# Attention stage of a hybrid decoder layer: a second PSUM bank for the value products, with the transpose buffers on three banks in place of four

## The chip, the cores and the metric

The kernel runs on one core of one Trainium2 chip. The metric is the device time of one execution in microseconds. Each of the core's engines has its own queue and takes its instructions in the order of the program: TensorE (PE in the profile; PEld is its weight load), VectorE (DVE), ScalarE (ACT), GpSimd (POOL) and SyncE (SP, here only for issuing transfers). Semaphores make one engine wait for another. PE writes its results to PSUM, of which the program uses eight banks of 512 float32 columns on 128 partitions; VectorE and ScalarE read them from there.

## The reference

One decoder layer: a mixture of dilated-window attention and pooling, a gated MLP with a short convolution, a gated embedding, and a final norm. The change touches the attention alone, which reduces to this:

```python
def _dilated_branch(q, k, v, slopes, window, dil):
    ...
    s = jnp.einsum('bnqrhd,bnkrhd->bnrhqk', qb, kk,
                   preferred_element_type=jnp.float32)
    ...
    s = s - slopes[:, None, None] * dist
    s = jnp.where(valid[:, None, None], s, -jnp.inf)
    m = jnp.max(s, axis=-1, keepdims=True)
    e = jnp.exp(s - m)
    den = jnp.sum(e, axis=-1)
    o = jnp.einsum('bnrhqk,bnkrhd->bnqrhd', e, vv.astype(jnp.float32))
    ...
def _dilated_attention(q, k, v, slopes):
    outs, maxes, dens = [], [], []
    for window, dil in DIL_PATTERNS:
        o, m, d = _dilated_branch(q, k, v, slopes, window, dil)
    ...
    w = d * jnp.exp(m - jnp.max(m, axis=0, keepdims=True))
    w = w / jnp.sum(w, axis=0, keepdims=True)
    return jnp.sum(w[..., None] * o, axis=0)
```

There are 8 heads of width 64, 2048 tokens, and three patterns (window, dilation): (128, 1), (512, 4), (2048, 16).

## The kernel before

The program has three stages on one core: projections (`phase_project`), attention (`phase_attention`), and the rest (`phase_rest`: output projection, MLP, gated embedding, final norm). Float32 values are carried as a high and a low part in the type float32r, so most products are made two or three times.

**Steps.** Attention runs over 128 steps: 8 heads of 16 query tiles of 128 tokens. Each step has a *near* part (dilation 1, 256 keys) and a *far* part that covers the two wider patterns together (128 to 512 keys). Four steps make a group, in which the far part has 512, 384, 256 and 128 keys in this order. Two heads make a pair.

**Order.** The order on every engine is written by hand. In tick s the loop goes through the list `CFG["ord"]`, and an entry with lag n works on step s-n. What matters here, in the order of the list:

- N, near scores of step s, two matmuls (L572, L573) into one half of the bank `sn`. Both halves belong to one tile and alternate by step.
- S, after the last step of a pair, the transposes of its statistics (`mix_stats`, or `last_near` for the last pair).
- o (lag 7), in every second tick: ScalarE copies half of the value result, `ev` (L659).
- F, far scores of step s, two matmuls (L561, L562) into `sf`, which has two banks.
- h (lag 2): ScalarE copies the transposed weights of step s-2 to their high part, `pth` (L613).
- nm: VectorE's near minimum of step s (L577).
- p (lag 7), in every second tick: the *fold*. VectorE adds the two halves of the value result (L660).
- fm: VectorE's far minimum (L583).
- l (lag 2): VectorE subtracts to get the low part of step s-2, `ptl` (L617).
- T (lag 1): PE transposes the exponentials of step s-1, three to six blocks of 128 columns (L600), into `tp`.
- V and W (lag 6): value products into the bank `o`: the far ones of a group (L642) in two ticks, then its near ones (L628) in two ticks. Every second tick starts a new result in `o`.
- ne, fe: ScalarE's exponentials of step s.

Instructions stand on their engine in this order, so on PE a tick reads N, F, T, V, W, and on VectorE nm, p, fm, l.

**PSUM.** The eight banks of the stage: `sn` one, `sf` two, `tp` four (two buffers of 1024 columns, of which a step uses up to 768), `o` one. A pool with `bufs=2` gives its tiles two places in turn, and whoever writes into a place waits until the tile before in that place has been read. Inside one tile the recording layer makes a write wait for earlier reads, and reads for earlier writes, as far as it takes them to touch the same memory. The statistics of a pair are transposed into a `tp` buffer (`tps`), and so are those of the last pair (`tpn`, `tpf`); these are then copied to SBUF by VectorE (L769, L771, L806) or ScalarE (L817).

Of the kernel before, what the change touches and what calls it, by code (L numbers as in the profile page):

```python
# [10 lines left out]
F32 = mybir.dt.float32  # L11
# [3 lines left out]
PSUM = bass.MemoryType.PSUM  # L15
DRAM = bass.MemoryType.DRAM

P = 128
# [5 lines left out]
NPAIR = H // 2  # L24
FF = 2816
NF = FF // P
CH = 512
# [27 lines left out]
def rdma(nc, dst, src):  # L55
    nc.sync.dma_start(fp(dst) if dst.dtype == F32R else dst, fp(src) if src.dtype == F32R else src)
# [429 lines left out]
def phase_attention(tc, g, mx, near_b, far_b):  # L486
# [3 lines left out]
    nc = tc.nc  # L490
    NS = H * NQ
    with ExitStack() as ctx:
        sb = ctx.enter_context(tc.tile_pool(name="b_sb", bufs=1, reuse_waits="tile"))
        ps_n = ctx.enter_context(tc.tile_pool(name="b_n", bufs=1, space=PSUM, reuse_waits="tile"))
        ps_f = ctx.enter_context(tc.tile_pool(name="b_f", bufs=2, space=PSUM, reuse_waits="tile"))
        ps_t = ctx.enter_context(tc.tile_pool(name="b_t", bufs=2, space=PSUM, reuse_waits="tile"))
        ps_o = ctx.enter_context(tc.tile_pool(name="b_o", bufs=1, space=PSUM, reuse_waits="tile"))

        heads, steps, groups, pairs = {}, {}, {}, {}

        def load_qk(h):
            t = heads[h] = Shared()
            pr, e = h // 2, h % 2
            rows = slice(DH * e, DH * e + DH)
            t.qhh = sb.tile([P, S], F32R, tag=f"qhh{e}", bufs=1, name=f"qhh{h}")
            t.qll = sb.tile([P, S], F32R, tag=f"qll{e}", bufs=1, name=f"qll{h}")
            t.qr = t.qhh.rearrange("p (c r) -> p r c", r=4)
            t.qlr = t.qll.rearrange("p (c r) -> p r c", r=4)
            t.ks = sb.tile([P, NCH, 4, P], F32R, tag=f"ks{e}", bufs=1, name=f"ks{h}")
            t.nb = sb.tile([P, 256], F32, tag=f"nb{e}", bufs=1, name=f"nb{h}")  # L510
            t.fb = sb.tile([P, 512], F32, tag=f"fb{e}", bufs=1, name=f"fb{h}")
            loads = []
            for half in range(2):
                hs = slice(half * DH, half * DH + DH)
                loads.append((t.qhh[hs], g.qh[pr][rows]))
                loads.append((t.ks[hs], (g.kh if half == 0 else g.kl)[pr][rows]))
                loads.append((t.qll[hs], g.ql[pr][rows]))
            loads += [(t.fb, far_b[h]), (t.nb, near_b[h])]
            return loads
# [5 lines left out]
        def load_v(pr, which, q):  # L525

            v = sb.tile([P, 4, 2, P], F32R, tag=which, bufs=4 + (which == "v1"), name=f"{which}_{pr}_{q}")
            vals[pr, which, q] = v
            src = near_v[:, 4 * q : 4 * q + 4, pr, :] if which == "v1" else far_v[q, :, :, pr, :]
            return v.rearrange("p b h d -> p b (h d)"), src  # L530
# [63 lines left out]

        def turn(s):
            st = steps[s]
            st.tp = ps_t.tile([P, 1024], F32, tag="t", name="tp")
            for b in range(2 - st.nb, 2 + st.nf):
                bs = slice(b * P, (b + 1) * P)
                nc.tensor.transpose(st.tp[:, bs], st.ee[:, bs], g.ident)  # L600
# [96 lines left out]
        def stats(s):  # L697
            if (s + 1) % (2 * NQ) == 0:
                pr = s // (2 * NQ)
                if pr < NPAIR - 1:  # L700
                    mix_stats(nc, g, mx, ps_t, pr, pairs[pr])
                else:
                    last_near(nc, g, mx, ps_t, pairs[pr])

        def mix(s):
            for pr in range(NPAIR - 1):
# [14 lines left out]
                    if d == CFG["m"][2] + CFG["m"][3] * c + CFG["m"][5]:  # L721
                        mix_store(nc, g, mx, nc.gpsimd, nc.gpsimd, pr, pairs[pr], c)()

        near_bank = []
        sel = mx.tile([8, NCH, 2, DH], F32R, tag="sel", name="sel")
        for c in range(NCH):
            nc.vector.tensor_copy(sel[:, c], g.ident[:8, c : 8 : NCH, None].to_broadcast([8, 2, DH]))
        with tc.manual_schedule(engines=set(EN.values())):
            for dst, src in load_qk(0):
                rdma(nc, dst, src)  # L730
            for q in range(4):
                for which in ("v3", "v1"):
                    rdma(nc, *load_v(0, which, q))
            queue = []
            stages = {
                "F": far_scores, "N": near_scores, "fm": far_max, "nm": near_max, "fe": far_exp, "ne": near_exp,
                "T": turn, "h": high, "l": low, "V": values, "W": values_b, "S": stats, "M": mix, "o": fold, "p": folded, "B": begin
            }
            for s in range(NS + 10):
                if s < NS:  # L740
                    h, n = divmod(s, NQ)
                    if n == 1 and h + 1 < H:
                        queue += load_qk(h + 1)
                    if queue:
                        rdma(nc, *queue.pop(0))
                    for pr in range(1, NPAIR):
                        if s - 2 * NQ * (pr - 1) in V_STEPS:
                            rdma(nc, *load_v(pr, *V_STEPS[s - 2 * NQ * (pr - 1)]))
                if s == NS + 2:
                    last_far(nc, g, mx, ps_t, pairs[NPAIR - 1])  # L750
                    pieces = pairs[NPAIR - 1].pieces = last_weights(nc, mx, pairs[NPAIR - 1])
                for nm, lag in CFG["ord"]:
                    if 0 <= s - lag < NS or nm == "M":
                        stages[nm](s - lag)
                for _ in range({NS + 3: 3, NS + 4: 2, NS + 5: 1}.get(s, 0)):
                    next(pieces)
# [1 line left out]
    return pairs[NPAIR - 1]  # L758


def mix_stats(nc, g, sb, psum, pr, pt):

    tp = psum.tile([P, 1024], F32, tag="t", name="tps")
    nc.tensor.transpose(tp[:64, :P], pt.st1.rearrange("p a e n -> p (a e n)"), g.ident)
    far = tp[:16, CH:].rearrange("p (c r) -> p r c", r=4)
    for r in range(4):
        nc.tensor.transpose(far[:, r, :], pt.st3[:, r].rearrange("p a e i -> p (a e i)"), g.ident)
    sx = sb.tile([64, P], F32, tag="sx", name="sx")
    nc.vector.tensor_copy(sx, tp[:64, :P])  # L769
    sy = sb.tile([16, CH], F32, tag="sy", name="sy")  # L770
    nc.vector.tensor_copy(sy, tp[:16, CH:])  # L771
    pt.sx, pt.sy = sx, sy


# [18 lines left out]

def last_near(nc, g, sb, psum, pt):

    near = psum.tile([P, 1024], F32, tag="t", name="tpn")
    for a in range(2):
        for m in range(4):
            nc.tensor.transpose(
                near[:8, a * CH + m * P : a * CH + (m + 1) * P],  # L800
                pt.st1[:, a].rearrange("p e (i m) -> p m e i", m=4)[:, m],
                g.ident,
            )
    pt.near = [sb.tile([16, CH], F32, tag="sy", name="nr")[:8], sb.tile([P, CH], F32, tag="m3", bufs=1, name="nr")[:8]]
    for a in range(2):
        nc.vector.tensor_copy(pt.near[a], near[:8, a * CH : (a + 1) * CH])  # L806


def last_far(nc, g, sb, psum, pt):
    far = psum.tile([P, 1024], F32, tag="t", name="tpf")  # L810
    for a in range(2):
        out = far[:8, a * CH : (a + 1) * CH].rearrange("p (j r) -> p r j", r=4)
        for r in range(4):
            nc.tensor.transpose(out[:, r, :], pt.st3[:, r, a].rearrange("p e i -> p (e i)"), g.ident)
    pt.far = [sb.tile([8, CH], F32, tag="fr", bufs=2, name="fr") for _ in range(2)]
    for a in range(2):
        nc.scalar.copy(pt.far[a], far[:8, a * CH : (a + 1) * CH])  # L817


def last_weights(nc, sb, pt):  # L820

    both = (pt.near, pt.far)
    lo = sb.tile([P, CH], F32, tag="m1", bufs=1, name="lo")[:8]
    nc.vector.tensor_tensor(lo, pt.near[0], pt.far[0], op=ALU.min)
    yield
    for mx_, _ in both:
        nc.vector.tensor_tensor(mx_, lo, mx_, op=ALU.subtract)
    yield
    for ex, _ in both:
        nc.scalar.activation(ex, ex, AF.Exp)  # L830
    yield
    for ex, dn in both:
        nc.vector.tensor_tensor(dn, ex, dn, op=ALU.mult)
    yield
    nc.vector.tensor_tensor(lo, pt.near[1], pt.far[1], op=ALU.add)
    yield
    nc.vector.reciprocal(lo, lo)
    yield
    pt.w = []
    for ex, _ in both:  # L840
        hi, low = (sb.tile([P, CH], F32R, tag=f"wb{y}", bufs=2, name=f"w{y}")[:8] for y in range(2))
        nc.vector.tensor_tensor(ex, ex, lo, op=ALU.mult)
        nc.scalar.copy(hi, ex)
        nc.vector.tensor_tensor(low, ex, fp(hi), op=ALU.subtract)
        pt.w.append((hi, low))
    yield
# [1040 lines left out]
```

## Time and profile before

| what | us |
|---|---|
| median of 3 runs (2516.77 to 2527.26) | 2523.27 |
| the profiled execution | 2522.12 |
| its span in the trace | 2519.8 |
| attention stage in it, first near scores to the last step's products and folds | about 335 |

The span reaches from the first to the last instruction of the profiled execution; about 2 us of its time lie around it. Over the whole span PE is busy 96% of the time, VectorE 63%, ScalarE 44%. These shares are averages over stages with different limits: in the attention stage the three engines are close to each other.

### The profile page before, as it was taken

To read this page: it belongs to the slowest core of one execution; us is meant where nothing else is said; L and a number is where in the kernel's file an instruction comes from. 1 tells how busy PE (TensorE), PEld (TensorE's weight loads), DVE (VectorE), ACT (ScalarE), POOL (GpSimd) and SP (SyncE) were. 2 spreads that over 40 slices of the span, in tenths; PEclk is the share of its full clock that TensorE was granted. 3 is DMA by queue.
4 is the path that set the end of the run, shared out by engine and by line. 5 is a ranking of instruction groups with operands and counts; after the bars stand their busy time and mean duration, and the time that the engine had idled before them with its cause. 6 is when DMAs were issued, how large, how long until landed. Compare 5 with 4: busy or idle time off the path is not lost.

```text
span 2519.8 us, 31897 instructions
## 1 busy us (share of the span) xinstructions
PE 2407.5 (96%) x11515; PEld 2022.4 (80%) x11515; DVE 1588.8 (63%) x2416; ACT 1108.6 (44%) x1923; POOL 515.7 (20%) x423
## 2 busy tenths in 40 slices
PE   8999998888779999999999999999999999999998
PEld 7888887777767877888887888888788888887888
DVE  6635427777774467888888666666535374435755
ACT  5423326887751135544446444444323242323322
POOL 3312221053430023333340000000122222221000
PEclk9999999999879999999999999999999999999999
DMA  7534358687646674555556334333546464635332
GB/s 240 174 120 180 142 178 248 166 193 180 164 164 221 223 252 167 167 177 181 175 194 211 122 117 138 121 114 117 191 134 222 149 219 150 208 122 173 124 105 88
DMA packets 209052, 424.08 MB, mean 168 GB/s; under 512 B 42464, under 2 KB 68896, under 8 KB 205824
## 3 DMA queue, kind: packets, MB, share of 16 engines
q1 hardware_dynamic: 170576, 368.41, 46.4%
q0 software_dynamic: 18672, 25.88, 3.1%
q10 hardware_dynamic: 19648, 27.77, 3.1%
q8 instruction: 90, 1.47, 0.2%
q14 instruction: 66, 0.54, 0.1%
HBM read 290.01 MB, written 131.89 MB: 167 GB/s over the span
## 4 chain that ended last, share of the span: by engine, by line
PE 79%; DMA 6%; DVE 6%; issue 3%; ACT 2%; POOL 0%; SPq 0%; ACTq 0%; POOLq 0%; DVEq 0%
PE ua L1315 18%; PE uc L1315 9%; PE dn L90 6%; PE dn L91 6%; PE dn L89 6%; PE ub L1315 4%; PE z L91 4%; PE z L89 4%; PE z L90 4%; PE o L89 2%; PE o L91 2%; PE o L90 2%; PE gp L89 2%; PE gp L91 2%; PE gp L90 2%
## 5 line engine op out<-in xcount | busy, mean ns | idle before, releaser
L89 PE MATMUL dn<-ah,hd 128*128 128x512 f32 x704 | 275.3, 391 | 2.8 <-ACT ah L84 2.8
L90 PE MATMUL dn<-al,hd 128*128 128x512 f32 x704 | 274.9, 391 | 1.7 <-DVE al L85 1.7
L91 PE MATMUL dn<-ah,ld 128*128 128x512 f32 x704 | 274.6, 390 | 0.0
L85 POOL TENSOR_TENSOR ld<-rd,hd 128x1024 fp32r<-128x1024 f32 x42 | 100.9, 2403 | 812.8 <-ACT hd L84 812.8
L84 ACT CAST hd<-rd 128x1024 fp32r<-128x1024 f32 x88 | 92.5, 1052 | 266.3 <-PE dn L90 230.9
L85 DVE TENSOR_TENSOR al<-ra,ah 128x512 fp32r<-128x512 f32 x88 | 116.8, 1330 | 136.0 <-ACT ah L84 136.0
L89 PE MATMUL z<-hnh,wh 128*128 128x512 f32 (+1 forms) x480 | 170.3, 355 | 9.9 <-ACT hnh L252 5.8
L90 PE MATMUL z<-hnl,wh 128*128 128x512 f32 (+1 forms) x480 | 170.0, 354 | 2.7 <-DVE hnl L253 2.6
L91 PE MATMUL z<-hnh,wl 128*128 128x512 f32 (+1 forms) x480 | 169.9, 354 | 2.3 <-POOL wl L85 1.7
L89 PEld LDWEIGHTS dn<-ah,hd 128*128 128x128 f32 x704 | 132.7, 188 | 31.0 <-ACT ah L84 3.2
L90 PEld LDWEIGHTS dn<-al,hd 128*128 128x128 f32 x704 | 132.7, 188 | 29.8 <-DVE al L85 2.2
L91 PEld LDWEIGHTS dn<-ah,ld 128*128 128x128 f32 x704 | 132.7, 189 | 27.4
L85 DVE TENSOR_TENSOR wu<-ru,wu 128x1024 fp32r<-128x1024 f32 x88 | 127.4, 1448 | 0.0
L155 DVE TENSOR_TENSOR acc<-acc,sq 128x512 f32<-128x512 f32 (+1 forms) x125 | 90.2, 722 | 47.6 <-ACT sq L154 34.6
L1315 PE MATMUL uc<-a22h,wu 128*128 128x512 f32 x352 | 115.7, 389 | 1.8 <-DVE uv L1338 1.8
L1315 PE MATMUL ua<-s2h,wu 128*128 128x512 f32 x352 | 115.8, 390 | 1.1 <-ACT ug L1452 1.1
L1315 PE MATMUL uc<-s3h,wu 128*128 128x512 f32 x352 | 116.2, 390 | 0.3 <-ACT s3h L1371 0.3
L1315 PE MATMUL ub<-a12h,wu 128*128 128x512 f32 x352 | 115.9, 390 | 0.3 <-ACT a12h L1371 0.3
L1315 PE MATMUL ua<-s4h,wu 128*128 128x512 f32 x352 | 115.5, 389 | 0.0
L1315 PE MATMUL ua<-s1h,wu 128*128 128x512 f32 x352 | 115.5, 389 | 0.0
L1315 PE MATMUL ua<-a11h,wu 128*128 128x512 f32 x352 | 115.5, 389 | 0.0
L85 DVE TENSOR_TENSOR ld<-rd,hd 128x1024 fp32r<-128x1024 f32 x46 | 56.2, 1223 | 89.1 <-ACT hd L84 89.1
(317 smaller groups left out, 6474.4 us busy)
## 6 DMA issues: line engine op xcount, KB each, us to landing
rd<-in_w_down_dram SPq DMA_DIRECT2D x88, 512.0 KB, 3.6
ru<-in_w_up_dram SPq DMA_DIRECT2D x66, 512.0 KB, 4.1
ra<-act SPq DMA_DIRECT2D x88, 256.0 KB, 3.8
act<-yg SPq DMA_DIRECT2D x43, 512.0 KB, 3.1
wr<-in_w_in_dram SPq DMA_DIRECT2D x64, 256.0 KB, 4.0
nt<-h SPq DMA_DIRECT2D x56, 256.0 KB, 3.9
h<-h SPq DMA_DIRECT2D x56, 256.0 KB, 5.6
td<-t SPq DMA_DIRECT2D x22, 512.0 KB, 2.6
```

The lines of the kernel that those rows point to most:

```text
L84: nc.scalar.copy(hi, src)
L85: (low or nc.gpsimd).tensor_tensor(lo, src, fp(hi), op=ALU.subtract)
L89: nc.tensor.matmul(ps, wh, ah, start=first, stop=False)
L90: nc.tensor.matmul(ps, wh, al, start=False, stop=False)
L91: nc.tensor.matmul(ps, wl, ah, start=False, stop=last)
L155: nc.vector.tensor_tensor(acc[:, :n], acc[:, :n], sq[:, :n], op=ALU.add)
L1315: nc.tensor.matmul(pst, x[:, ksl], y, start=first and k == 0 and n == 0, stop=k == HK - 1 and n == 2, skip_group_check=True)
```

## The change

The pool of the transpose buffers, `ps_t`, goes from two buffers of 1024 columns to a single tile of 1536 columns, three banks, which is made once. Even steps write its columns 0 to 767, odd steps 768 to 1535. The bank that this frees goes to the value products: `ps_o` now has two places, taken in turn. A pair's statistics are transposed into columns 768 to 1535 of that tile, and the last pair's into two tiles of the far-score pool `ps_f`. Nothing is computed differently.

```diff
-        ps_t = ctx.enter_context(tc.tile_pool(name="b_t", bufs=2, space=PSUM, reuse_waits="tile"))
-        ps_o = ctx.enter_context(tc.tile_pool(name="b_o", bufs=1, space=PSUM, reuse_waits="tile"))
+        ps_t = ctx.enter_context(tc.tile_pool(name="b_t", bufs=1, space=PSUM, reuse_waits="tile"))
+        ps_o = ctx.enter_context(tc.tile_pool(name="b_o", bufs=2, space=PSUM, reuse_waits="tile"))
...
         def turn(s):
             st = steps[s]
-            st.tp = ps_t.tile([P, 1024], F32, tag="t", name="tp")
+            if not turned:
+                turned.append(ps_t.tile([P, 1536], F32, tag="t", name="tp"))
+            st.tp = turned[0][:, s % 2 * 768 : s % 2 * 768 + 768]
...
-                    mix_stats(nc, g, mx, ps_t, pr, pairs[pr])
+                    mix_stats(nc, g, mx, turned[0][:, 768:], pr, pairs[pr])
                 else:
-                    last_near(nc, g, mx, ps_t, pairs[pr])
+                    last_near(nc, g, mx, ps_f, pairs[pr])
...
-                    last_far(nc, g, mx, ps_t, pairs[NPAIR - 1])
+                    last_far(nc, g, mx, ps_f, pairs[NPAIR - 1])
...
-    near = psum.tile([P, 1024], F32, tag="t", name="tpn")
+    near = [psum.tile([P, CH], F32, tag="f", name="tpn") for _ in range(2)]
...
-    far = psum.tile([P, 1024], F32, tag="t", name="tpf")
+    far = [psum.tile([P, CH], F32, tag="f", name="tpf") for _ in range(2)]
```

No instruction is added, removed or moved on any engine; what changes is what they wait for. On PE, in the middle of the stage, one tick and the start of the next value result stand like this before (`sn`, `sf`: scores; `tp`: transposes of `ee`; `o`: value products; in brackets the semaphores that a row waits for, named by the engine or transfer queue that raises them):

```order
L562 MATMUL sf<-ks_4667,qll_4666 128x256
L600 MATMUL tp<-ident,ee 128x128 [waits DVE_49,PE_49,Activation_49]
L600 MATMUL tp<-ident,ee 128x128
L600 MATMUL tp<-ident,ee 128x128 [waits Activation_49]
L600 MATMUL tp<-ident,ee 128x128 x2
L642 MATMUL o<-pth,v_1_3_4753 128x512 [waits DMAHW5_49,DVE_49]
```

The same place of the changed kernel:

```order
L562 MATMUL sf<-ks_4635,qll_4634 128x256
L602 MATMUL tp<-ident,ee 128x128 [waits DVE_49]
L602 MATMUL tp<-ident,ee 128x128
L602 MATMUL tp<-ident,ee 128x128 [waits Activation_49]
L602 MATMUL tp<-ident,ee 128x128 x2
L644 MATMUL o<-pth,v_1_3_4718 128x512 [waits DMAHW7_49,PE_49]
```

The value product no longer waits for VectorE; the first transpose does, now for VectorE alone. The rows don't tell for which of VectorE's instructions. On VectorE the order is the same in both kernels; two ticks of the changed one, from near minimum (`tt`, `st` from `sn`) over fold (`s` from `o`) and far minimum (from `sf`) to the low part (`ptl`):

```order
L577 ISA tt,st_5502<-sn,nb_5069 128x256 [waits DVE_49,PE_49]
L577 ISA st_5502 128x1
L662 TENSOR_TENSOR s_4596<-o,ev 64x512 [waits Activation_49]
L583 ISA tt,st_5503<-sf,fb_5070 128x256 [waits PE_49]
L583 ISA st_5503 128x1
L619 TENSOR_TENSOR ptl<-tp,pth 128x768 [waits Activation_49]
L577 ISA tt,st_5502<-sn,nb_5069 128x256 [waits DVE_49,PE_49]
L577 ISA st_5502 128x1
L583 ISA tt,st_5503<-sf,fb_5070 128x128 [waits PE_49]
L583 ISA st_5503 128x1
L619 TENSOR_TENSOR ptl<-tp,pth 128x640 [waits Activation_49]
```

Nothing moved here: the low part stays the last of VectorE's work in a tick.

More of the change, by code (lines that the diff above doesn't have):

```diff
@@ L722, in mix @@
                         mix_store(nc, g, mx, nc.gpsimd, nc.gpsimd, pr, pairs[pr], c)()
-        near_bank = []
+        near_bank, turned = [], []
         sel = mx.tile([8, NCH, 2, DH], F32R, tag="sel", name="sel")
@@ L758, in phase_attention, with mix_stats @@
     return pairs[NPAIR - 1]
-def mix_stats(nc, g, sb, psum, pr, pt):
-    tp = psum.tile([P, 1024], F32, tag="t", name="tps")
+def mix_stats(nc, g, sb, tp, pr, pt):
     nc.tensor.transpose(tp[:64, :P], pt.st1.rearrange("p a e n -> p (a e n)"), g.ident)
-    far = tp[:16, CH:].rearrange("p (c r) -> p r c", r=4)
+    far = tp[:16, 256:].rearrange("p (c r) -> p r c", r=4)
     for r in range(4):
@@ L770, in mix_stats @@
     sy = sb.tile([16, CH], F32, tag="sy", name="sy")
-    nc.vector.tensor_copy(sy, tp[:16, CH:])
+    nc.vector.tensor_copy(sy, tp[:16, 256:])
     pt.sx, pt.sy = sx, sy
@@ L799, in last_near @@
             nc.tensor.transpose(
-                near[:8, a * CH + m * P : a * CH + (m + 1) * P],
+                near[a][:8, m * P : (m + 1) * P],
                 pt.st1[:, a].rearrange("p e (i m) -> p m e i", m=4)[:, m],
@@ L805, in last_near @@
     for a in range(2):
-        nc.vector.tensor_copy(pt.near[a], near[:8, a * CH : (a + 1) * CH])
+        nc.vector.tensor_copy(pt.near[a], near[a][:8])
 def last_far(nc, g, sb, psum, pt):
-    far = psum.tile([P, 1024], F32, tag="t", name="tpf")
+    far = [psum.tile([P, CH], F32, tag="f", name="tpf") for _ in range(2)]
     for a in range(2):
-        out = far[:8, a * CH : (a + 1) * CH].rearrange("p (j r) -> p r j", r=4)
+        out = far[a][:8].rearrange("p (j r) -> p r j", r=4)
         for r in range(4):
@@ L816, in last_far @@
     for a in range(2):
-        nc.scalar.copy(pt.far[a], far[:8, a * CH : (a + 1) * CH])
+        nc.scalar.copy(pt.far[a], far[a][:8])
 def last_weights(nc, sb, pt):
```

## The prediction

> **What bounds the kernel now.** I read the page first, then the busy time by stretches, then the timeline of the attention stage, the one stage that the change touches.
>
> ```profile
> span 2519.8 us, 31897 instructions
> ...
> 399.00:733.70 334.70, 273.79 (x1673) 246.66 (x1671) 255.38 (x748) 260.61 (x713) 109.51 (x116) 0.91 0.71 175
> 513.30:547.90 34.60, 31.44 (x209) 28.69 (x207) 30.18 (x89) 31.93 (x90) 20.32 (x21) 1.00 0.88 207
> ```
>
> The columns behind a stretch are its length, the busy time of PE, PEld, DVE, ACT and POOL with their instruction counts, the granted PE clock and the DMA share. The stage takes 334.7 of 2519.8 us. The second stretch is one head of 16 steps that no transfer disturbs: 34.6 us, or 2.16 us a step, with ACT busy 31.93, PE 31.44 and DVE 30.18 us. Three engines are all close to full: they work on different steps at the same time, and none has slack to spend. That overlap is what the change puts at risk.
>
> ```profile
> 399.11 0.28 PE L572 MATMUL sn<-ks,qhh 128*128 128x256 f32 x1
> ...
> 714.65 0.29 PE L572 MATMUL sn<-ks,qhh 128*128 128x256 f32 x1
> ```
>
> These are the near scores of the first and the last step: 127 steps in 315.5 us. At 2.16 us they would take 274, so some 41 us are stalls at head changes, nearly all on loads.
>
> Inside a step, PE runs near scores (L572, L573), far scores (L561, L562), the transposes of the step before (L600), then value products of a much earlier step (L642 or L628). DVE runs near minimum (L577), in every second step the fold (L660), far minimum (L583), and the low part of the transposes of two steps back (L617). Here are two neighbouring steps, one with a fold and one without; columns are start, duration, engine, line, operation, and in brackets idle time and what ended it.
>
> ```profile
> 544.09 0.42 DVE L577 CUSTOM_DVE_ANT_0 tt<-sn,nb 128x256 f32<-128x256 f32 x1 [0.32 <-PE sn L573]
> ...
> 544.67 0.69 DVE L660 TENSOR_TENSOR s<-o,ev 64x512 f32<-64x512 f32 x1 [0.15 <-ACT ev L659]
> ...
> 545.42 0.50 PE L642 MATMUL o<-pth,v 128*128 128x512 f32 x1 [0.36 <-DVE s L660]
> ...
> 545.75 0.95 DVE L617 TENSOR_TENSOR ptl<-tp,pth 128x768 fp32r<-128x768 f32 x1
> ...
> 546.79 0.42 DVE L577 CUSTOM_DVE_ANT_0 tt<-sn,nb 128x256 f32<-128x256 f32 x1
> ...
> 547.00 0.62 PE L600 MATMUL tp<-ident,ee 128*128 128x128 f32 x4
> ...
> 547.38 0.36 PE L642 MATMUL o<-pth,v 128*128 128x256 f32 x1
> 547.41 0.82 DVE L617 TENSOR_TENSOR ptl<-tp,pth 128x640 fp32r<-128x640 f32 x1
> ...
> 548.04 0.28 PE L573 MATMUL sn<-ks,qll 128*128 128x256 f32 x1
> ```
>
> At 547.00 the transposes run, while the low part of an earlier step is read only at 547.41: the transposes don't wait for it, since it reads the other buffer. At 545.42 the first product into the single value bank waits for the fold. That second wait is what the change takes away.
>
> **The change part by part.** *The shared bank.* The two transpose buffers become the halves 0 to 767 and 768 to 1535 of one tile. A bank of this program has 512 columns, so columns 512 to 1023, the middle bank, belong to both halves. The question is whether writing one half waits for reads of the other. The nearest case in this trace is the near-score bank, whose two halves also alternate by step:
>
> ```profile
> 401.33 0.41 DVE L577 CUSTOM_DVE_ANT_0 tt<-sn,nb 128x256 f32<-128x256 f32 x1
> ...
> 401.80 0.39 PE L572 MATMUL sn<-ks,qhh 128*128 128x256 f32 x1 [1.69 <-DVE st L577]
> ```
>
> The scores of the second step go to the other half of that bank, and still PE idled 1.69 us until the first step's minimum had read its own half. So waits go by bank within a tile. The Trainium skill, page "PSUM — Partial Sum Buffer", section on bank collisions, says the same: two engines must be kept apart by bank and not by address. By that rule the wait below exists; if addresses decided, it would not, and the first rival below would hold.
>
> What the transposes of step s-1 then wait for is the low part of step s-2, which stands last in DVE's order of the very same step: near minimum, fold, far minimum, low part. The far minimum needs the far scores that PE issues just ahead of these transposes. And the products and the next near scores stand behind the transposes on PE. So the work closes into a ring: transposes, products and near scores on PE; then near minimum, fold, far minimum and low part on DVE; then the next transposes. PE and DVE no longer overlap, except for the far scores.
>
> The ring for the two steps above, at full clock:
> - DVE, from near minimum to the end of the low part: 544.09 to 545.75 + 0.95, 2.61 us; and 546.79 to 547.41 + 0.82, 1.44 us. The 0.15 us that the fold waited for ACT goes, as ACT's copy gets time during the new idle. Together 3.90 us.
> - PE, transposes: four blocks from 547.00 to the product at 547.38, 0.095 us each; nine blocks in the two steps are 0.86 us.
> - PE, from first product to the next near minimum: 545.42 to 546.79, 1.37 us; 547.38 to the second near matmul's end, 548.04 + 0.28, plus 0.04 us as from PE to DVE elsewhere, 0.98 us. Together 2.35 us.
> - Hand-over from DVE to PE: the fold ends at 545.36, the product starts at 545.42, 0.06 us, twice.
>
> Sum 0.86 + 2.35 + 3.90 + 0.12 = 7.23 us for two steps, 3.6 us a step in place of 2.16. ACT's work (31.93 us a head, 2.0 us a step) stays hidden beside it.
>
> *The clock.* A ring in which PE does 3.2 us of 7.23, and the far scores beside (some 0.45 us a step), keeps PE busy about 57%. What the granted clock does then is shown by windows of 3.41 us, the grid on which it changes:
>
> ```profile
> 400.22:403.63 3.41, 1.63 (x9) 1.38 (x10) 3.12 (x13) 1.85 (x7) 1.51 (x3) 1.00 0.91 363
> 403.63:407.04 3.41, 3.41 (x19) 3.41 (x18) 2.18 (x10) 3.29 (x10) 0.00 (x0) 0.50 0.76 221
> ...
> 564.06:567.47 3.41, 3.04 (x13) 2.95 (x14) 2.34 (x7) 2.17 (x7) 1.45 (x3) 0.50 1.02 224
> 567.47:570.88 3.41, 3.17 (x22) 2.85 (x21) 2.67 (x9) 3.25 (x10) 0.00 (x0) 1.00 1.12 271
> 584.54:587.95 3.41, 2.79 (x10) 2.08 (x10) 2.78 (x9) 3.14 (x9) 0.78 (x1) 0.50 0.07 14
> 587.95:591.36 3.41, 3.41 (x17) 3.34 (x16) 1.68 (x6) 1.80 (x6) 2.42 (x3) 0.50 0.19 31
> ...
> 2294.62:2298.03 3.41, 1.91 (x9) 1.22 (x7) 1.23 (x1) 1.97 (x3) 0.00 (x0) 1.00 0.78 251
> 2298.03:2301.44 3.41, 1.62 (x6) 1.06 (x7) 1.22 (x1) 1.54 (x2) 0.00 (x0) 1.00 1.01 326
> ```
>
> PE busy 1.63 us of a window was followed by half clock; 1.91 us was not. At half clock, 3.04 us brought the full clock back, 2.79 us did not. A fold step leaves PE idle for over 2 us in a row, so windows under 1.7 us come within every few steps and the clock falls. At half clock PE's own work is longer:
>
> ```profile
> 404.73 1.27 PE L600 MATMUL tp<-ident,ee 128*128 128x128 f32 x5
> 405.65 0.46 PE L572 MATMUL sn<-ks,qhh 128*128 128x128 f32 x1
> ```
> ```profile
> 586.23 0.80 PE L642 MATMUL o<-pth,v 128*128 128x512 f32 x1 [0.62 <-DVE s L660]
> ...
> 588.11 0.41 PE L573 MATMUL sn<-ks,qll 128*128 128x256 f32 x1
> ```
>
> Five transposes take 0.92 us, 0.184 each; the product chain to the end of the near scores, plus 0.04, takes 2.33 us in place of 1.37, a factor of 1.70. Two steps become 9 x 0.184 + 2.35 x 1.70 + 3.90 + 0.12 = 9.68 us, 4.84 a step. PE is then busy about two thirds of the time, short of what brings the full clock back, except where a window happens to cover PE's longest unbroken run (0.92 + 2.33 + 0.45 us in the heaviest step). I estimate about one window in six at full clock. Mixed by time, two steps take 1 / (5/6 / 9.68 + 1/6 / 7.23) = 9.16 us, 4.58 a step.
>
> A rule speaks against the half clock. The Trainium skill, page "TensorE: Matmul & The Clock Gate", section "Part 1: The HAM clock gate", says that the clock falls after at least one idle window of some 3.4 us; no gap of the ring is that long, so by it the clock would stay full, which is the second rival. The first window above disagrees: its longest PE gap was 1.69 us.
>
> *The sum.* 127 x 4.58 = 582 us, less 6 because the first six steps have no products, is 576 where 315.5 stood: +260. The 41 us of load stalls are taken as gone, since loads then have twice the time; they are the upper bound.
>
> *The second value bank.* Products no longer wait for the fold, but stand behind transposes that wait for the low part, which is behind that fold on DVE. Inside the ring it is worth nothing. In the last steps, without scores, it counts:
>
> ```profile
> 725.35 0.80 PE L642 MATMUL o<-pth,v 128*128 128x512 f32 x1 [2.47 <-DVE s L660]
> ...
> 729.41 0.58 PE L628 MATMUL o<-pth,v 128*128 128x256 f32 x1 [1.45 <-DVE s L660]
> ```
>
> That is at most -3.9 us. *Statistics* are the same transposes and copies, in other banks. A pair's end puts its copies into the ring, at worst some 1 us three times; the last pair's go to score banks that are idle by then. From -3.9 to +3 us for both edits; I take -2.
>
> From the profiled execution's 2522.1 us: 2522.1 + 260 - 2 = **2780 us**. The median of the runs shown, 2523.27, is 0.05% above it, which changes nothing here.
>
> **The rivals.**
> 1. *The halves do not wait for each other*, because the dependence goes by address. Then the wait at 545.42 goes and nothing comes in its place. ACT is next: 31.93 of 34.60 us. A head could lose at most 2.7 us, eight heads 21 us: 2501 us. It decides as soon as transposes start before the preceding low part ends. Against it stands the wait at 401.80.
> 2. *The ring, but at full clock.* 127 x 3.615 - 4 = 455 us, +140 - 2: 2660 us. For it: windows of the lighter steps hold more than 1.91 us of work. Against it: 1.63 us of 3.41 was enough for half clock, and the fold steps have such windows.
> 3. *The ring at half clock throughout*: 127 x 4.84 - 7 = 608 us, 2812 us; with all 41 us of stalls left, 2853 us. For it: few windows hold 3.04 us. Against the stalls: DMA was busy 0.71 of a stage that gets much longer.
>
> **How the numbers follow.** Forecast (ring, mostly half clock) 0.65; full clock 0.18; half clock throughout or stalls left 0.12; halves independent 0.05. The range leaves out only that last case: from under the full-clock ring, 2650, to the last case with its stalls, 2850. All ring cases are slower by far more than 0.5%, about the least that a measurement of this kernel can tell from no change: slower 0.95. The independent halves give mostly a gain of over 0.5%: faster 0.04, within 0.5% 0.01.
>
> **What would show it.** Right: in the profile after, the transposes' idle time ends on the low part, in nearly every step, some 128 times and over 1 us each; the waits for the fold in front of the products are gone; PE's clock in the stage is near 0.6; and near scores of neighbouring steps lie some 4.6 us apart. A clock near 1.0 with steps of 3.6 us is the second rival. Transposes that overlap the low part before them would make the whole prediction wrong, as would a stage in which DVE is still busy above 70%.

## The result, and the profile after

The changed kernel takes 2716.49 us (median of 4 runs, 2714.10 to 2717.79) beside 2522.39 us for the kernel before: a ratio of 1.0776, interval 1.0759 to 1.0794. It is 194 us slower; 258 were forecast (2780, range 2650 to 2850).

The first near scores to the last, as stretches of the trace. Columns: stretch, length, busy us of PE, PEld, DVE, ACT and POOL with instruction counts, granted PE clock, DMA share, GB/s. First the kernel before, then the changed one:

```profile
399.11:714.65 315.54, 262.37 (x1614) 237.58 (x1612) 242.74 (x729) 252.20 (x697) 109.40 (x116) 0.93 0.75 183
```
```profile
398.93:911.65 512.72, 320.41 (x1613) 277.64 (x1612) 242.13 (x729) 263.77 (x698) 108.44 (x115) 0.76 0.43 113
```

The same number of instructions takes 197 us longer. VectorE has the same 242 us of work, now 47% of the stretch in place of 77%. PE's busy time grew by 58 us without one more matmul: its clock was lower, 0.76 in the mean. The loss lies here: from the last near scores to the next stage's first matmul it is 17.1 us in place of 19.1, and the two whole executions differ by 194.

What that time was spent on is in the list of waits of this stage (who waited for whom, us in total, times, longest):

```profile
DVE tt L577 <- PE sn L573: 249.3, 122, 3.3
PEld tp L602 <- DVE ptl L619: 227.5, 125, 3.2
PE tp L602 <- DVE ptl L619: 190.4, 125, 2.8
```

PE's transposes wait for VectorE's low part in 125 steps, 1.5 us each in the mean; VectorE's near minimum waits for PE's near scores in 122 steps, 2.0 us each. The two engines take turns. In the kernel before, no wait of the transposes for the low part was among the longest, and the list of the stage had these rows:

```profile
PE o L628 <- DVE s L660: 23.3, 30, 4.8
...
DVE tt L577 <- PE sn L573: 23.1, 45, 1.7
...
PE o L642 <- DVE s L660: 14.6, 29, 2.5
```

The products' waits for the fold (L660, now L662) are gone from the list. One round of the turns on the timeline, at half clock:

```profile
670.86 0.42 DVE L577 CUSTOM_DVE_ANT_0 tt<-sn,nb 128x256 f32<-128x256 f32 x1 [2.49 <-PE sn L573]
...
671.41 0.69 DVE L662 TENSOR_TENSOR s<-o,ev 64x512 f32<-64x512 f32 x1
672.14 0.69 DVE L583 CUSTOM_DVE_ANT_0 tt<-sf,fb 128x512 f32<-128x512 f32 x1
...
672.76 0.69 DVE L619 TENSOR_TENSOR ptl<-tp,pth 128x512 fp32r<-128x512 f32 x1
...
673.50 0.69 PE L602 MATMUL tp<-ident,ee 128*128 128x128 f32 x2 [1.82 <-DVE ptl L619]
673.84 0.56 PE L630 MATMUL o<-pth,v 128*128 128x256 f32 x1
...
675.48 0.41 PE L573 MATMUL sn<-ks,qll 128*128 128x256 f32 x1
...
675.93 0.42 DVE L577 CUSTOM_DVE_ANT_0 tt<-sn,nb 128x256 f32<-128x256 f32 x1 [2.49 <-PE sn L573]
```

The low part ends at 673.45 and the transposes start at 673.50; the near scores end at 675.89 and the near minimum starts at 675.93. Between 670.86 and 675.93 the two engines hand over twice and share no time except for the far scores.

### The profile page after: what moved, and what is told of

It reads as the page before. It is cut to its first block, busy times and chain, and to the rows that moved or that the text cites. A ratio compares the mean times of both kernels' runs of the same rounds, so it can differ in the third digit from the quotient of the medians.

```text
span 2714.0 us, 31830 instructions
## 1 busy us (share of the span) xinstructions
PE 2462.1 (91%) x11515; PEld 2061.8 (76%) x11515; DVE 1591.4 (59%) x2416; ACT 1119.2 (41%) x1923; POOL 514.3 (19%) x423
## 4 chain that ended last, share of the span: by engine, by line
PE 59%; DVE 2%; issue 2%; DMA 1%; ACT 0%; POOL 0%; SPq 0%; POOLq 0%; DVEq 0%; ACTq 0%
PE ua L1316 16%; PE uc L1316 8%; PE dn L90 6%; PE dn L89 6%; PE dn L91 6%; PE ub L1316 4%; PE o L91 2%; PE o L89 2%; PE o L90 2%; PE gp L89 2%; PE gp L91 2%; PE gp L90 2%; PE pl L91 1%; PE pl L89 0%; PE pl L90 0%
## 5 line engine op out<-in xcount | busy, mean ns | idle before, releaser
L602 PE MATMUL tp<-ident,ee 128*128 128x128 f32 x568 | 117.7, 348 | 194.2 <-DVE ptl L619 194.0
L602 PEld LDWEIGHTS tp<-ident,ee 128*128 128x128 f32 x568 | 79.2, 174 | 232.0 <-DVE ptl L619 231.5
L577 DVE CUSTOM_DVE_ANT_0 tt<-sn,nb 128x256 f32<-128x256 f32 (+1 forms) x128 | 53.2, 416 | 252.7 <-PE sn L573 252.7
```

The lines of the kernel that those rows point to most:

```text
L577: nc.vector.tensor_tensor_reduce(st.tt[:, st.ns], st.nv, st.t.nb[:, 256 - st.wn :], 1.0, BIG, ALU.add, ALU.min, st.nm1)
```

## The experiments

Each kernel ran beside the kernel before on the same chip; ratios are to it, with their 95% interval. The distance from the first to the last near scores (127 steps) is taken from each profile.

**own_banks.** Does the wait come from the shared bank?

```diff
-        ps_o = ... name="b_o", bufs=2
+        ps_o = ... name="b_o", bufs=1
...
-                turned.append(ps_t.tile([P, 1536], F32, tag="t", name="tp"))
-            st.tp = turned[0][:, s % 2 * 768 : s % 2 * 768 + 768]
+                turned.append(ps_t.tile([P, 2048], F32, tag="t", name="tp"))
+            st.tp = turned[0][:, s % 2 * 1024 : s % 2 * 1024 + 768]
```

The statistics move along with the second half, to columns 1024 and up, and are spread over its two banks.

> The changed kernel, but with the two transpose halves 1024 columns apart, so that no bank belongs to both (four banks again), and one value bank again; still one tile, and the statistics still where the change put them. Theory of the shared bank (transposes wait for the low part of the step before, because both halves touch the middle bank): with the bank goes the wait, so about the time of the kernel before, 2522 us, 2510 to 2535; steps about 2.2 us apart. Rival, the single tile (a write into one half waits for every read of the tile, whatever the bank): about 2716 us. Rival, the statistics in other banks: also far above 2522.

Measured: 2724.34 us, ratio 1.0803 (1.0787 to 1.0819). The shared-bank theory falls. No bank belongs to both halves any more, and the wait is still there:

```profile
DVE tt L577 <- PE sn L573: 249.2, 122, 3.3
PEld tp L602 <- DVE ptl L619: 231.0, 127, 3.2
PE tp L602 <- DVE ptl L619: 193.7, 127, 2.8
```

Left over are the single tile and the statistics, which this kernel also has in their new place.

**two_tiles.** Two tiles in place of two halves of one, all else as in own_banks:

```diff
-            if not turned:
-                turned.append(ps_t.tile([P, 2048], F32, tag="t", name="tp"))
-            st.tp = turned[0][:, s % 2 * 1024 : s % 2 * 1024 + 768]
+            if len(turned) < 2:
+                turned.append(ps_t.tile([P, 1024], F32, tag=f"t{s % 2}", name="tp"))
+            st.tp = turned[s % 2][:, :768]
```

> As own_banks, but the two transpose halves are two tiles of 1024 columns, each made once, in place of the halves of one tile of 2048. Banks, addresses' spacing, statistics and the single value bank are the same. New theory, the wait goes by the whole tile: a write into either half of one tile waits for all earlier reads of that tile, whatever bank they touch; with two tiles the wait is two steps back again: 2522 us, 2510 to 2535. Rival, what is made once and never handed back makes the waits, or the statistics do: 2720 us as own_banks.

Measured: 2520.47 us, ratio 0.9996 (0.9981 to 1.0010), the time of the kernel before. In its list of waits the transposes don't appear among the longest; the products wait for the fold again:

```profile
PEld o L630 <- DVE s L662: 35.2, 31, 6.0
PE o L630 <- DVE s L662: 27.7, 31, 5.8
```

With own_banks this settles the cause. The recording layer makes a write into one half wait for the reads of the whole tile, in whatever bank they are. "As far as it takes them to touch the same memory", in the section on the kernel before, therefore means more here than common bytes or a common bank. The two tiles are also made once and never handed back, so that is not the cause. The run clears the statistics as well: they are in the changed place here, at no cost that can be measured.

**one_value_bank.** The changed kernel with `ps_o` at `bufs=1`.

> The changed kernel with one value bank in place of two, the rest as changed (seven banks used). Theory: inside the ring the second bank is worth nothing, since the transposes ahead of the products wait for a later instruction of VectorE than the fold; only the last steps, without scores, lose their 3.9 us again: 2720 us, 2716 to 2726. Rival, the second bank pays in the ring too and hides part of the loss: 2735 us or more.

Measured: 2724.70 us, ratio 1.0801 (1.0781 to 1.0822). That is 8 us above the changed kernel, of which 4 were expected; the two were timed on different chips, beside 2519.76 and 2522.39 us of the kernel before. In the ring the second value bank is worth little: the steps are 4.04 us apart in both. Most of the 8 us stands behind the last near scores: from there to the next stage's first matmul the profile of one_value_bank has 23.1 us, at a clock of 0.50, where the changed kernel has 17.1 at 0.89. So part of it is the clock that these last steps happened to get, and not the bank.

**filler.** How much of the loss is the clock? One value bank, and four matmuls that fill PE's idle time in each step:

```diff
         def turn(s):
...
+            if not spare:
+                spare.append(ps_x.tile([P, CH], F32, tag="x", name="spare"))
+            for i in range(4):
+                nc.tensor.matmul(spare[0], g.onesr, st.t.qhh[:, i * CH : (i + 1) * CH], start=True, stop=True)
```

> The changed kernel with one value bank, and with four extra matmuls of 128x512 per step (0.23 us each at full clock) into the bank that is left over, between the far scores and the transposes, where PE idles; their results are not used. Theory that about a quarter of the loss is the half clock, which held 47% of the stage: the fillers raise PE's busy share to over 80%, the clock stays full, steps take 3.5 us all along, the stage some 60 us less than in one_value_bank: 2660 us, 2640 to 2680, clock near 1.0 in the stage. Rival, the clock is only a by-product and the ring takes 4.0 us a step anyway: the same as one_value_bank, about 2720 us, or more by what the fillers delay the transposes.

Measured: 2658.97 us, ratio 1.0546 (1.0530 to 1.0561). The stage in one_value_bank, then in filler:

```profile
400.07:913.66 513.59, 322.07 (x1614) 278.42 (x1613) 242.15 (x729) 263.74 (x698) 108.59 (x115) 0.76 0.43 113
```
```profile
399.40:851.60 452.20, 377.64 (x2118) 307.43 (x2117) 243.04 (x729) 262.89 (x698) 109.02 (x116) 0.99 0.49 129
```

With 504 more matmuls in these records the stage is 61 us shorter, at a clock of 0.99 in place of 0.76. So the half clock is worth some 61 us, perhaps a little more, as the fillers may have delayed some transposes: PE waited for the low part in 106 steps here and in 127 without them. The ring at full clock is the rest, 452 us where 315.5 stood.

**low_part_first.** The wait stays, but the instruction that releases it comes earlier: `['l', 2]` moves ahead of `['nm', 0]` in the order of a tick.

> The changed kernel, banks and waits included, but VectorE takes the low part of step s-2 at the start of a tick, ahead of the near minimum, in place of at its end. The transposes still wait for that low part, but it no longer stands behind this tick's scores. Theory of the ring: it opens; what is left is transposes (0.43 us mean), high part on ScalarE (0.63), low part (0.74) and three hand-overs, some 2.1 us a step, no longer than ScalarE's own work of 2.0 to 2.2: steps of 2.2 to 2.6 us, 2535 us, 2515 to 2580. Rival, the shared bank itself costs the time (any wait between neighbouring steps, or engines on one bank slowing each other): still above 2650 us.

Measured: 2668.12 us, ratio 1.0585 (1.0565 to 1.0605). The forecast was missed and the time fell on the rival's side, above 2650: 48 us came back where 181 were hoped for, with steps of 3.63 us at a clock of 0.86. The rows show what was overlooked:

```profile
DVE ptl L619 <- ACT pth L615: 213.3, 125, 3.7
PEld tp L602 <- DVE ptl L619: 198.2, 121, 2.8
...
ACT ee L589 <- DVE st L577: 151.4, 124, 1.8
```

The low part now waits for the high part. That stands in ScalarE's queue behind the exponentials of the step before. The first of these waits for VectorE's near minimum in 124 steps, and the near minimum now stands behind the low part. The ring had moved to another engine. What speaks against the rival is the next pair of runs.

**short_ring** and **short_ring_before.** The order of a tick is changed on three engines, so that only transposes, high part and low part are in the ring; once on the changed kernel, once on the kernel before (the list in short form, each entry with its lag):

```diff
-    'ord': B 0, M 0, N 0, S 1, o 7, F 0, h 2, nm 0, p 7, fm 0, l 2, T 1, V 6, W 6, ...
+    'ord': B 0, M 0, T 2, N 0, S 1, h 2, o 7, F 0, nm 0, l 2, p 7, fm 0, V 6, W 6, ...
```

> The changed kernel with its banks and its one tile, and another order: the transposes one step later and first on PE in a tick, the high part first on ScalarE, the low part on VectorE right behind the near minimum. In low_part_first the ring still ran through ScalarE's queue: low part, near and far minimum, far exponentials, and only behind them the next high part. Here it is transposes, high part, low part alone: 0.43 + 0.63 + 0.74 us and hand-overs, 2.2 us a step, beside ScalarE's 2.0 to 2.2: 2545 us, 2515 to 2600. Rival, any wait between neighbouring steps costs over a us a step wherever it stands: above 2640 us.

> The kernel before with the order of short_ring alone, as its control: without the one tile the order should matter little, 2520 us, 2505 to 2545. If it is itself above 2545, that part of short_ring's time is the order's and not the wait's.

Measured: 2573.63 us, ratio 1.0208 (1.0194 to 1.0221), and 2617.67 us, ratio 1.0382 (1.0367 to 1.0397). With the same banks and the same tile, an order gives back 143 of the 194 us. So the wait between neighbouring steps does not cost over a microsecond wherever it stands; it costs what stands in front of the instruction that ends it. The control went wrong: the order is itself bad for the kernel before, by 97 us, and better with the change than without. Its near minimum waits for the near scores 96 times, 121 us, where 45 times and 23 us stood, and its fold comes later in a tick, with the one value bank behind it; short_ring has two. How much of short_ring's remaining 53 us is order and how much is the wait stays open, since the two kernels also differ in the number of value banks.

**one_score_bank.** The second value bank, paid for elsewhere. On the kernel before:

```diff
-        ps_f = ... name="b_f", bufs=2
-        ps_o = ... name="b_o", bufs=1
+        ps_f = ... name="b_f", bufs=1
+        ps_o = ... name="b_o", bufs=2
```

> The kernel before, with the bank for the second value result taken from the far scores (one bank in place of two) and the transpose buffers left alone. Theory: the far scores of a step then wait for the far minimum of the step before, which is done long before PE gets there, and the products no longer wait for the fold (38 us of PE idle time before in the stage); ScalarE, busy 92% of a head, is next: 2505 us, 2495 to 2520. Rival, the far scores' new wait takes back what the fold's wait gave: 2515 to 2540. Second rival, ScalarE bounds the stage already, so nothing moves: 2522.

Measured: 2510.37 us, ratio 0.9958 (0.9945 to 0.9971): below both kernels, 0.42% under the kernel before. One head of it, as a window:

```profile
509.48:542.57 33.09, 31.43 (x208) 29.02 (x207) 29.31 (x89) 31.27 (x90) 17.77 (x19) 1.00 0.93 210
```

And in its list of waits, the one that took the fold's place:

```profile
PEld sf L561 <- DVE st L583: 41.2, 36, 13.0
```

The head takes 33.1 us in place of 34.6, with ScalarE busy 95% of it. The far scores now wait for the far minimum, 36 times; one of these waits is 13 us long, the others come to 28 us.

**fold_after_low** and **fold_after_low_before.** One more step on that path: the entry `['p', 7]` moves behind `['l', 2]`, on one_score_bank and, as a control, on the kernel before.

> one_score_bank (one far-score bank, two value banks, transposes as before the change) with the fold moved on VectorE from between the near and far minimum to behind the low part. Theory: with the second value bank nobody waits for the fold within its tick, so it may go last; the far minimum comes 0.7 us earlier in every second step, and with it the far scores of the next step, which in one_score_bank waited some 35 us in the stage for it: 2500 us, 2490 to 2512. Rival, ScalarE is the bound and only passes the time on: the same as one_score_bank, 2510.

> The kernel before with the same move of the fold, as control. With one value bank the first product of every second step waits for the fold, which now comes about 1.3 us later in the tick: slower than before, 2560 us, 2535 to 2600. Rival, the fold's place does not matter: 2521 us.

Measured: 2516.11 us, ratio 0.9982 (0.9968 to 0.9996), and 2622.87 us, ratio 1.0396 (1.0372 to 1.0421). Nothing was gained over one_score_bank, the ratio is if anything a little higher; the rival comes closer. The low part now waits for ScalarE's high part:

```profile
DVE ptl L617 <- ACT pth L613: 44.2, 53, 6.0
```

The control lost 103 us where some 40 were expected. It has a row that the theory did not count:

```profile
DVE tt L577 <- PE sn L573: 140.8, 106, 2.4
```

With one value bank and a late fold, PE and VectorE take turns here as well: the near scores stand behind products that wait for the fold, and the near minimum waits for them in 106 steps. The clock in this stage is 0.83, so part of the 103 us is the clock.

## Why the prediction was right, and where it was not

**The ring: right.** Transposes, products and near scores on PE, then near minimum, fold, far minimum and low part on VectorE, with nothing beside them but the far scores and ScalarE. The rows of after show both hand-overs in nearly every step, as the last part of the prediction asked. Its price was right too: 3.6 us a step at full clock was forecast, and filler, at a clock of 0.99 and with its extra matmuls, measured 452.2 / 127 = 3.56.

**Why the ring is there: wrong.** The step "So waits go by bank within a tile" failed. The row that it rested on, the near scores at 401.80 waiting for the other half's reader, fits waits by bank and waits by tile equally well, since both halves of that tile lie in one bank. own_banks and two_tiles tell them apart: it is the tile. The number did not suffer, because the change has both, a shared bank and a single tile. That was luck: by the prediction's rule own_banks would have been as fast as the kernel before. The sentence on the Trainium skill, page "PSUM — Partial Sum Buffer", section on bank collisions, was used for more than it states: it says what the engines must not do at the same time, and not by what the waits of this program are drawn. No run here shows what two halves that share a bank would need if they were two tiles.

**The clock: right in kind, mis-sized.** The prediction asked for a clock near 0.6 and steps of 4.6 us; 0.76 and 4.04 were measured. The term that failed is "about one window in six at full clock". The mean clock of 0.76 is half clock for 48% of the stretch, not five sixths. With that share, the prediction's own step times give 1 / (0.48 / 4.84 + 0.52 / 3.615) = 4.11 us a step, and 127 x 4.11 - 5 = 518 us against 513. So the step times hold, and the share alone makes 58 of the 63 us by which the forecast of the stage, 576 us, was too high. Windows of the changed kernel on the grid of its clock show why:

```profile
601.52:604.93 3.41, 2.03 (x13) 1.63 (x12) 1.82 (x6) 1.94 (x6) 0.00 (x0) 1.00 1.09 215
604.93:608.35 3.42, 1.91 (x12) 1.65 (x12) 1.88 (x6) 1.80 (x6) 0.00 (x0) 1.00 0.59 154
615.17:618.59 3.42, 2.23 (x14) 1.77 (x13) 1.94 (x8) 1.85 (x6) 3.27 (x6) 1.00 0.13 54
618.59:622.00 3.41, 1.46 (x11) 1.47 (x11) 2.03 (x5) 2.09 (x6) 3.33 (x3) 1.00 0.93 287
622.00:625.41 3.41, 2.28 (x11) 1.88 (x11) 1.30 (x5) 1.31 (x4) 3.27 (x5) 0.50 0.03 7
...
645.89:649.31 3.42, 2.86 (x11) 2.67 (x12) 0.51 (x1) 0.96 (x3) 0.00 (x0) 0.50 0.00 0
649.31:652.72 3.41, 2.28 (x18) 2.08 (x18) 1.44 (x5) 1.48 (x5) 0.00 (x0) 1.00 0.55 142
```

On this grid all 149 windows of the stretch have a clock of either 0.50 or 1.00: 70 the one, 79 the other. PE's work in a window was forecast well, 57% at full clock and two thirds at half clock, against 56% and 70% in the mean. Too low was the estimate of how often the half clock ends. Of the 79 windows at full clock, 21 were followed by half clock; of the 69 at half clock that have a next one, 20 were followed by full clock. With falls as frequent as that, one window in six at full clock would need a return after one in 19. The prediction had bounds for both on its page, 1.63 and 1.91 us for the fall, 2.79 and 3.04 us for the return, but did not count how many windows of a ring with mixed steps lie above them.

**The second rival, full clock throughout,** gave 2660 us, and filler, which nearly forces it, took 2659; as filler has one value bank and the extra matmuls, an agreement to 1 us is partly luck. The changed kernel lies between this rival and the forecast, 56 us above the one and 64 below the other. The Trainium skill's rule on the clock (page "TensorE: Matmul & The Clock Gate", section "Part 1: The HAM clock gate") does not hold here: PE's longest wait in this stage for the low part was 2.8 us, for its weight loads 3.2, shorter than the idle window of some 3.4 us that the page asks for, and the clock still fell for half of the time.

**Load stalls: right.** They were taken as gone; the DMA share fell from 0.75 to 0.43, and no transfer stands among the longest waits of PE, VectorE or ScalarE. The second to the seventh head now take 64.7 to 66.8 us each; before, the loads spread them from 34.6 to 51.2.

**The second value bank and the statistics: right.** -2 us was taken for the end of the stage, and 19.1 us became 17.1; that it fits so well is partly luck, as the clock there was 0.67 before and 0.89 after. one_value_bank shows that the bank brings little inside the ring, two_tiles that the statistics cost nothing that can be measured. The first rival, in which the fold's wait goes and nothing takes its place, was given up to 21 us of gain; one_score_bank, the nearest to it that ran, gained 10.

## What to carry to other kernels

Before two buffers become parts of one tile, find out by what the program's waits are drawn: here by the tile, so that a wait for work two steps back became a wait for the step before, although the bytes, and in own_banks even the banks, were apart. A wait costs what stands in front of the instruction that ends it: the same tile cost 194 us with the low part last on its engine, and 53 with another order. When two full engines begin to take turns, price the clock as well, by the busy share of single windows and not by the mean, and count the windows that bring it back as well as those that bring it down.

## What the runs showed of the hardware

PE can be made faster by giving it more to do: 504 matmuls whose results are not used made the stage 61 us shorter, about as filler's expectation had it.

The 149 windows of 3.41 us in the changed kernel's stage narrow the two bounds of the clock, as far as their records are complete. At full clock, all windows with 1.62 us of PE work or less were followed by half clock and all with 1.79 us or more by full clock; in between both occur. At half clock, 2.74 us or more brought the full clock back and 2.64 us or less did not. These bounds are not sharp for every stage: in the kernel before, a window with 1.83 us in the last steps was followed by half clock, and 2.79 us did not bring the full clock back.
